# Moving three GpSimd fills ahead of the key and query fills in a hybrid decoder trunk

## The chip, the cores and the metric

The kernel runs on one core of a Trainium2 chip. The metric is the device time of one execution in microseconds, as the median of several runs; the kernel before was run three times. Besides these times there is a trace of one execution, taken by the hardware profiler. In it PE is TensorE's matmuls, PEld its weight loads (they overlap the matmuls), DVE is VectorE, ACT is ScalarE, POOL is GpSimd, and SP is SyncE, whose queue issues nearly all DMAs. "L1217" is line 1217 of the kernel.

## The reference

Two layers of a decoder trunk on 512 tokens plus 16 learned meta tokens (L = 528), with 1024 channels, in float32. Each layer is a mixer and a feed-forward part. The mixer reads one input projection of the normed input and runs three groups beside each other; the change lies in the attention group with its forget gate.

```python
def forgetting_attention(q, k, v, log_f):
    scale = ATTN_HEAD_DIM ** -0.5
    F = jnp.cumsum(log_f, axis=1).transpose(0, 2, 1)

    def attend(start, end):
        qb = q[:, start:end]
        s = jnp.einsum("bqhd,bkhd->bhqk", qb, k[:, :end],
                       preferred_element_type=jnp.float32) * scale
        s = s + F[:, :, start:end, None] - F[:, :, None, :end]
        mask = jnp.arange(start, end)[:, None] >= jnp.arange(end)[None, :]
        s = jnp.where(mask, s, NEG_INF)
        p = jax.nn.softmax(s, axis=-1)
        return jnp.einsum("bhqk,bkhd->bqhd", p.astype(v.dtype), v[:, :end])
    ...

def mixer_sublayer(h, pre_g, post_g, w_in, b_forget, ...):
    u = rms_norm(h, pre_g)
    z = jnp.einsum("bld,de->ble", u, w_in)
    q, k, v, f_logit, a_val, a_gate, sc_b, sc_c, sc_x = jnp.split(z, idx, axis=-1)
    log_f = jax.nn.log_sigmoid((f_logit + b_forget).astype(jnp.float32))
    y_attn = forgetting_attention(q.reshape(hs), k.reshape(hs), v.reshape(hs), log_f)
    a = a_val * jax.nn.sigmoid(a_gate)
    a = causal_depthwise_conv(a, a_dw_w) + a_dw_b
    a = jax.nn.silu(layer_norm(a, a_ln_g, a_ln_b))
    y_conv = jnp.einsum("blc,ce->ble", a, a_pw_w)
    y_sc = sc_b * causal_depthwise_conv(sc_c * sc_x, sc_conv_w)
    y = jnp.concatenate([y_attn, y_conv, y_sc], axis=-1)
    y = jnp.einsum("ble,ed->bld", head_rms_norm(y, head_g), w_out)
    return h + rms_norm(y, post_g)
```

There are 8 heads of 64 channels. The feed-forward part is a gated convolution network with 2816 channels.

## The kernel before

**Tiling.** Channels lie on the 128 partitions, tokens along the free dimension, cut into two halves of 264. Every float32 product is made of three products of rounded parts: a weight is split into a rounded high part (`whi`, a ScalarE cast, L622 in the mixer) and the rest (`wlo`, a VectorE subtraction, L626), the normed input likewise into `uhi` and `ulo`; `mm3` (L650) issues the three matmuls (L656). Weights come through three raw buffers by DMAs on SP's queue (L618).

**Order.** In the mixers the orders of TensorE, ScalarE, VectorE and GpSimd are written out: a planner (`Flow`) holds an estimated duration for each operation, runs threads of TensorE work and queues of work of the other engines against each other in its own time, and issues each instruction when its turn comes. `every` (L1820) names the four engines whose issue order is kept as it is. DMAs on SP's queue pass through the same planner (`flow.op("sp", ...)`), but SP is not in `every`. The setup fills at the head of a mixer are issued directly and have no duration in the planner.

**The mixer around the change** (`mixer`, L944). It opens with the convolution gates and the first products of the short convolution. Then the pool `ap` is opened (L1065) in the memory that the wide weight tiles of the first products used, so that a tile of `ap` waits for the last matmul that reads a weight tile lying there. Its tiles lie in the order of their first mention. In that order of the code GpSimd fills:

- `vals` (L1157 to L1159), the V tiles with their columns of ones;
- `causal` (L1161 to L1164), the mask for the diagonal;
- for each of four head slots, the auxiliary rows of the key tile `kh` (two fills) and of the query tile `qh` (two fills), L1178 to L1184: these rows carry the gate and the maxima through the logits' matmul;
- the first columns of the two `dm` tiles (L1185 to L1189), the diagonal matrices of the maxima;
- `fx` (L1190 and L1191), the forget gate's input, 128 × 5 × 8; `gt` is made there, but not filled;
- the two `p4` tiles (L1195 to L1197), which take the exponentials of the last 16 keys.

Fills through the helper `mset` show as L418.

**Who reads them.** `fill` (L1634) runs the projections in a fixed order: V half 0 with the forget gate's columns (`v_proj`, L1202), then q 0, k 0, a short convolution product, q 1 and so on. `v_proj` makes five tiles of up to 128 tokens (matmuls on L1228), which take turns in three PSUM banks; for each, ScalarE copies V out (L1213) and VectorE adds the bias and writes `fx[:, b, :]` (L1217). A bank is free when both have read it. The thread `forget_gate` (L1244) then follows: ScalarE's Abs, Exp and Ln (L1248 to L1250), VectorE's negative part and sum (L1251, L1253), four additions into `fpre` (L1256), TensorE's prefix sum with two matmuls (L1260 on `fe`, L1261 on `fpre`), VectorE's copy to `gt` (L1262), five transposes (L1270), the split into high and low rows (L1274, L1276), and DMAs of these rows into the key tiles (`gate_rows`, L1287, which show as L533). `maxima` (L1398) reads the key tiles with these rows (L1414).

On VectorE's queue the planner puts the taps of the 31-wide convolution (L972) and of the short one (L1029) between these steps; ScalarE's writes of q and k into their tiles (L1333) and VectorE's of the low parts (L1338) follow the projections.

Of the kernel before, what the change touches and what calls it, by code (L numbers as in the profile page):

```python
# [9 lines left out]
F32 = mybir.dt.float32  # L10
# [5 lines left out]
P = 128  # L16
# [3 lines left out]
N_META = 16  # L20
H = L // 2
DEPTH = 2
HEADS = 8
# [337 lines left out]
def tile_hybrid_trunk(ctx: ExitStack, tc: tile.TileContext, xT, wflat, pv_d, out):  # L361
    nc = tc.nc
# [3 lines left out]
    def T(pool, shape, dt, tag, bufs=None):  # L366
        uid[0] += 1
        kw = {} if bufs is None else {"bufs": bufs}
        return pool.tile(list(shape), dt, tag=tag, name=f"{tag}_{uid[0]}", **kw)
# [47 lines left out]
    def mset(t, val):  # L417
        nc.gpsimd.memset(t.bitcast(F32), val)  # L418
# [525 lines left out]
    def mixer(l, ypool, first, close_first, spans, front=None, rz0=None):  # L944
# [120 lines left out]
        ap = ms.enter_context(tc.tile_pool(name=f"ap{l}", bufs=1, side="right", reuse_waits="tile"))  # L1065
# [91 lines left out]
        vals = T(ap, [P, 5, HEADS, VW], F32, "vals")  # L1157
        mset(vals[:, 4], 0.0)
        mset(vals[:, :, :, DH:], 1.0)  # L1159

        causal = T(ap, [P, 400], BF16, "causal")  # L1161
        nc.gpsimd.memset(causal, 0.0)
# [23 lines left out]
        for j in range(2):  # L1186
            dm = T(ap, [P, L], F32R, f"dm{j}")
            mset(dm[:, :N_META], 0.0)
            dms.append(dm)  # L1189
        fx = T(ap, [P, 5, HEADS], F32, "fx")  # L1190
        nc.gpsimd.memset(fx, 0.0)  # L1191
        gt = T(ap, [P, 5, HEADS], F32, "gt")
        g_hl = [T(mp, [P, L], F32, "sq", 2)[:HEADS].bitcast(F32R) for _ in range(2)]

        p4 = [T(ap, [P, N_META], F32, f"p4{i}") for i in range(2)]  # L1195
        for t in p4:
            mset(t, 0.0)  # L1197


        v_at = {}  # L1200

# [690 lines left out]
    for l in range(DEPTH):  # L1892
# [15 lines left out]
        with ms, tc.manual_schedule(engines=every):  # L1908
            flow.yields = YM
            y, y_at, early = mixer(l, ypool, first, wxs.close, i_spans, front, rz0)  # L1910
# [177 lines left out]
```

## Time and profile before

| | us |
|---|---|
| median of 3 runs | 1301.95 |
| lowest and highest of the 3 | 1300.68 and 1302.20 |
| the profiled execution | 1301.88 |
| its span, first to last instruction | 1300.2 |
| granted TensorE clock, mean of the span | 0.997 of full speed |
| layer 0: from the V products to the gate's rows | about 49.7 to 79 us |
| layer 1: the same | about 696 to 726 us |

A row of a timeline gives the start, the time taken, the engine, the line, the operation with output and inputs, the shape, and in brackets how long the engine had stood idle before and what released it. Rows of one kind that follow each other are merged, with their number behind the x. A row of the waits gives who waited for whom, the total in us, how many times, and the longest. TensorE's matmuls overlap: each is shown with some 0.28 us, while their starts are 0.12 us apart, so lost time is read from the starts.

### The profile page before, as it was taken

To read this page: it belongs to the slowest core of one execution; us is meant where nothing else is said; L and a number is where in the kernel's file an instruction comes from. 1 tells how busy PE (TensorE), PEld (TensorE's weight loads), DVE (VectorE), ACT (ScalarE), POOL (GpSimd) and SP (SyncE) were. 2 spreads that over 40 slices of the span, in tenths; PEclk is the share of its full clock that TensorE was granted. 3 is DMA by queue.
4 is the path that set the end of the run, shared out by engine and by line. 5 is a ranking of instruction groups with operands and counts; after the bars stand their busy time and mean duration, and the time that the engine had idled before them with its cause. 6 is when DMAs were issued, how large, how long until landed. Compare 5 with 4: busy or idle time off the path is not lost. (4 is left out here: it accounts for less than half of the span.)

```text
span 1300.2 us, 23941 instructions
## 1 busy us (share of the span) xinstructions
PE 1278.3 (98%) x9802; PEld 1226.7 (94%) x9802; DVE 852.7 (66%) x1449; ACT 612.2 (47%) x1143; POOL 96.2 (7%) x254
## 2 busy tenths in 40 slices
PE   8999999999999999999989999999999999999997
PEld 8999899999999999999989998899999799989997
DVE  7798765687624663566676877757786256636664
ACT  7254577654423432344662645866543234314443
POOL 1313311000000000000003133100000000000000
PEclk9999999999999999999989999999999999999999
DMA  6136132502232222223340361334032332232321
GB/s 238 34 100 158 50 99 78 201 18 98 82 98 83 96 79 101 95 83 100 105 142 18 108 166 43 97 125 147 18 103 92 97 88 89 72 122 86 92 72 65
DMA packets 46637, 124.75 MB, mean 96 GB/s; under 512 B 5616, under 2 KB 15984, under 8 KB 46528
## 3 DMA queue, kind: packets, MB, share of 16 engines
q1 hardware_dynamic: 46480, 123.10, 30.7%
q8 instruction: 77, 1.26, 0.4%
q14 instruction: 32, 0.26, 0.1%
q0 software_dynamic: 48, 0.13, 0.0%
HBM read 108.04 MB, written 4.33 MB: 86 GB/s over the span
## 5 line engine op out<-in xcount | busy, mean ns | idle before, releaser
L656 PE MATMUL psum<-uhi,whi 128*128 128x264 f32 (+1 forms) x1936 | 454.9, 287 | 2.8 <-ACT uhi L837 1.1
L656 PE MATMUL psum<-ulo,whi 128*128 128x264 f32 (+1 forms) x1936 | 449.2, 285 | 0.8 <-DVE ulo L1869 0.4
L656 PE MATMUL psum<-uhi,wlo 128*128 128x264 f32 (+1 forms) x1936 | 447.3, 284 | 0.0
L656 PEld LDWEIGHTS psum<-uhi,whi 128*128 128x128 f32 x1936 | 324.0, 189 | 8.2 <-issue 1.9
L656 PEld LDWEIGHTS psum<-ulo,whi 128*128 128x128 f32 x1936 | 325.0, 189 | 1.9 <-DVE ulo L1869 0.6
L656 PEld LDWEIGHTS psum<-uhi,wlo 128*128 128x128 f32 x1936 | 324.8, 189 | 0.0
L656 PE MATMUL psum<-yhi,whi 128*128 128x264 f32 (+3 forms) x888 | 247.7, 302 | 1.4 <-ACT yp L2020 1.0
L656 PE MATMUL psum<-yhi,wlo 128*128 128x264 f32 (+3 forms) x888 | 245.4, 299 | 0.7 <-DVE wlo L626 0.7
L656 PE MATMUL psum<-ylo,whi 128*128 128x264 f32 (+3 forms) x888 | 245.0, 298 | 0.0
L508 ACT CAST whi<-raw 128x1024 fp32r<-128x1024 f32 (+1 forms) x110 | 113.3, 1031 | 214.7 <-PE psum L656 200.3
L509 DVE TENSOR_TENSOR wlo<-raw,whi 128x1024 fp32r<-128x1024 f32 (+1 forms) x110 | 132.0, 1200 | 81.7 <-ACT whi L508 79.7
L656 PEld LDWEIGHTS psum<-yhi,whi 128*128 128x128 f32 x888 | 159.0, 188 | 8.7 <-ACT yp L2020 1.4
L656 PEld LDWEIGHTS psum<-yhi,wlo 128*128 128x128 f32 x888 | 159.1, 188 | 6.4 <-DVE wlo L626 1.1
L656 PEld LDWEIGHTS psum<-ylo,whi 128*128 128x128 f32 x888 | 159.3, 188 | 5.4
L1969 DVE SCALAR_TENSOR_TENSOR c<-z,pv,c 128x528 f32<-128x528 f32 (+1 forms) x176 | 131.9, 756 | 2.7
L626 DVE TENSOR_TENSOR wlo<-raw,whi 128x1024 fp32r<-128x1024 f32 (+2 forms) x86 | 102.5, 1204 | 33.6 <-ACT whi L622 30.9
L622 ACT CAST whi<-raw 128x1024 fp32r<-128x1024 f32 (+2 forms) x86 | 87.9, 1030 | 31.1 <-PE psum L656 19.7
L972 DVE SCALAR_TENSOR_TENSOR cacc<-apad,pv,cacc 128x528 f32<-128x528 f32 x120 | 87.6, 771 | 0.2
L1987 ACT CAST yhi<-c 128x528 fp32r<-128x528 f32 (+1 forms) x44 | 27.6, 627 | 108.6 <-DVE c L1983 108.6
L1979 ACT ACTIVATE c<-c 128x528 f32<-128x528 f32 (+1 forms) x44 | 28.1, 639 | 79.3 <-DVE c L1969 79.3
L1967 ACT ACTIVATE c<-z,pv 128x528 f32<-128x528 f32 (+1 forms) x88 | 63.3, 726 | 0.4 <-DVE z L1935 0.4
L1932 DVE TENSOR_TENSOR z<-psum,rz 128x528 f32<-128x528 f32 x40 | 28.3, 708 | 53.7 <-PE psum L656 52.2
(214 smaller groups left out, 1417.2 us busy)
## 6 DMA issues: line engine op xcount, KB each, us to landing
raw<-in_w_dram SPq DMA_DIRECT2D x160, 512.0 KB, 3.6
raw<-in_w_dram SPq DMA_DIRECT2D x32, 448.0 KB, 3.5
h<-in_x_dram SPq DMA_DIRECT2D x16, 264.0 KB
q<-pair_hi SPq DMA_DIRECT2D x24, 132.0 KB, 2.2
k<-pair_hi SPq DMA_DIRECT2D x24, 132.0 KB, 2.4
raw<-in_w_dram SPq DMA_DIRECT2D x4, 528.0 KB, 3.4
h_dram<-h SPq DMA_DIRECT2D x4, 528.0 KB
h<-h_dram SPq DMA_DIRECT2D x8, 264.0 KB, 5.8
```

The source lines that it names most:

```text
L508: nc.scalar.copy(hi[:, :sz], raw[:, :sz])
L509: nc.vector.tensor_sub(lo[:, :sz], raw[:, :sz], hi[:, :sz].bitcast(F32))
L622: nc.scalar.copy(box["hi"][:, :sz], box["raw"][:, :sz])
L626: nc.vector.tensor_sub(lo[:, :sz], box["raw"][:, :sz], box["hi"][:, :sz].bitcast(F32))
L656: nc.tensor.matmul(d, lhsT=w[a][:, k, cols], rhs=rhs(b, k, hf), start=start and i == 0 and p == 0, stop=stop and i == n - 1 and p == 2)
L972: nc.vector.scalar_tensor_tensor(conv[j], in0=src, in1=conv[j], scalar=col("a_dw_w", CK * j + i), op0=ALU.mult, op1=ALU.add)
L1932: nc.vector.tensor_mul(two(t[:, off:]), srcs[0], two(rz))
L1967: nc.scalar.activation(dst, src[:, 2:2 + 2 * fw], AF.Copy, scale=wtap(2, t))
L1969: nc.vector.scalar_tensor_tensor(dst, in0=src[:, i:i + 2 * fw], scalar=wtap(i, t), in1=dst, op0=ALU.mult, op1=ALU.add)
L1979: silu = nc.scalar.activation(cs[0], cs[0], AF.Silu)
L1987: nc.scalar.copy(ghi, cs[0])
```

## The change

The allocation and fill of `fx`, the allocation of `gt`, and the allocation and fills of the two `p4` tiles move from behind the fills of `dm` to a place right behind the fills of `vals`. GpSimd's order becomes vals, fx, p4, causal, keys and queries, dm. The tiles of `ap` between the old and the new place (causal, the key and query tiles, dm) lie 448 bytes further on in every partition. It is done once in each layer's mixer.

```diff
         vals = T(ap, [P, 5, HEADS, VW], F32, "vals")
         mset(vals[:, 4], 0.0)
         mset(vals[:, :, :, DH:], 1.0)
+        fx = T(ap, [P, 5, HEADS], F32, "fx")
+        nc.gpsimd.memset(fx, 0.0)
+        gt = T(ap, [P, 5, HEADS], F32, "gt")
+        p4 = [T(ap, [P, N_META], F32, f"p4{i}") for i in range(2)]
+        for t in p4:
+            mset(t, 0.0)
 
         causal = T(ap, [P, 400], BF16, "causal")
...
             dm = T(ap, [P, L], F32R, f"dm{j}")
             mset(dm[:, :N_META], 0.0)
             dms.append(dm)
-        fx = T(ap, [P, 5, HEADS], F32, "fx")
-        nc.gpsimd.memset(fx, 0.0)
-        gt = T(ap, [P, 5, HEADS], F32, "gt")
         g_hl = [T(mp, [P, L], F32, "sq", 2)[:HEADS].bitcast(F32R) for _ in range(2)]
-
-        p4 = [T(ap, [P, N_META], F32, f"p4{i}") for i in range(2)]
-        for t in p4:
-            mset(t, 0.0)
-
 
         v_at = {}
```

## The prediction

> **What bounds the kernel now.** I read the page's busy shares first, then the waits of the whole trace, then the timelines of GpSimd, VectorE, ScalarE and TensorE around the one wait that touches the moved fills.
>
> ```profile
> span 1300.2 us, 23941 instructions
> PE 1278.3 (98%) x9802; PEld 1226.7 (94%) x9802; DVE 852.7 (66%) x1449; ACT 612.2 (47%) x1143; POOL 96.2 (7%) x254
> ```
>
> TensorE is busy for 98% of the span, so an edit can gain only what TensorE itself stands still for: 1300.2 − 1278.3 = 21.9 us over the whole run, and only the part of it that this edit reaches. The waits show where that part can be. The first row is from the waits of all engines, the others are those of TensorE's weight loads (PEld) and matmuls (PE); the columns are the total in us, the number of times, the longest.
>
> ```profile
> DVE fx L1217 <- POOL p L418: 12.2, 2, 6.3
> PE psum L1261 <- DVE fpre L1256: 1.7, 2, 0.9
> PEld psum L1261 <- DVE fpre L1256: 2.0, 2, 1.0
> PEld psum L1270 <- DVE gt L1262: 0.6, 2, 0.3
> PEld psum L1228 <- DVE fx L1217: 0.3, 2, 0.2
> PEld psum L1414 <- DVE mcol L1421: 1.0, 3, 0.6
> ```
>
> VectorE stands still for 12.2 us, once in each layer's mixer, ahead of the first addition into the forget gate's input tile (fx, L1217), because GpSimd has not filled that tile yet. Three small TensorE waits hang on the same chain: the V products for a bank (L1228), the gate's prefix sum (L1261), the gate's transposes (L1270). GpSimd in layer 0, then VectorE (columns: start, us, engine, line, operation):
>
> ```profile
> 45.65 1.10 POOL L418 MEMSET vals<- 128x528 f32 x2
> ...
> 49.76 1.11 POOL L418 MEMSET q<- 32x528 f32 x2 [1.11 <-PE psum L656]
> ...
> 58.14 0.14 POOL L1191 MEMSET fx<- 128x40 f32 x1
> ```
>
> ```profile
> 46.55 3.52 DVE L972 SCALAR_TENSOR_TENSOR cacc<-apad,pv,cacc 128x528 f32<-128x528 f32 x5
> ...
> 51.60 0.75 DVE L1027 TENSOR_SCALAR sccx<-cxp,pv 128x528 f32<-128x528 f32 x1
> 58.31 0.17 DVE L1217 TENSOR_TENSOR fx<-psum,pv 128x8 f32<-128x8 f32 x1 [5.96 <-POOL p L418]
> ...
> 60.63 2.12 DVE L972 SCALAR_TENSOR_TENSOR cacc<-apad,pv,cacc 128x528 f32<-128x528 f32 x3
> ...
> 68.42 2.34 DVE L626 TENSOR_TENSOR wlo<-raw,whi 128x1024 fp32r<-128x1024 f32 x2
> ...
> 70.90 0.87 DVE L1338 SCALAR_TENSOR_TENSOR q<-psum,q 64x264 fp32r<-64x264 f32 x2
> 71.81 0.77 DVE L1256 TENSOR_TENSOR fpre<-fpre,fe 128x8 f32<-128x8 f32 x4
> ...
> 73.51 1.23 DVE L626 TENSOR_TENSOR wlo<-raw,whi 128x1024 fp32r<-128x1024 f32 x1
> 74.77 0.20 DVE L1262 COPY gt<-psum 128x40 f32<-128x40 f32 x1
> ```
>
> The reader is to see that fx is filled at 58.14, behind all fills of the key and query tiles, and that VectorE's next instruction starts 0.03 us after that fill ends (58.14 + 0.14 = 58.28). ScalarE and TensorE over the same stretch:
>
> ```profile
> 52.78 0.37 ACT L1213 COPY vals<-psum 128x256 f32<-128x256 f32 x1 [2.91 <-PE psum L1228]
> ...
> 64.70 0.36 ACT L1213 COPY vals<-psum 16x256 f32<-16x256 f32 x1 [2.59 <-PE psum L1228]
> 67.14 0.24 ACT L1248 ACTIVATE fe<-fx 128x40 f32<-128x40 f32 x1 [2.07 <-DVE fx L1217]
> 67.28 1.03 ACT L622 CAST whi<-raw 128x1024 fp32r<-128x1024 f32 x1
> ...
> 69.52 0.77 ACT L1333 ACTIVATE q<-psum 64x264 fp32r<-64x264 f32 x2
> 70.50 0.80 ACT L1333 ACTIVATE q<-psum 64x264 fp32r<-64x264 f32 x2 [0.22 <-PE psum L656]
> 71.32 1.05 ACT L622 CAST whi<-raw 128x1024 fp32r<-128x1024 f32 x1
> ```
>
> ```profile
> 58.30 0.28 PE L1228 MATMUL psum<-wlo,uhi 128*128 128x264 f32 x1
> 58.53 0.39 PE L1228 MATMUL psum<-whi,uhi 128*128 128x264 f32 x1
> 58.76 0.28 PE L1228 MATMUL psum<-whi,ulo 128*128 128x264 f32 x1
> 58.88 0.28 PE L1228 MATMUL psum<-wlo,uhi 128*128 128x264 f32 x1
> ...
> 71.39 0.31 PE L1260 MATMUL psum<-fe,tri 128*128 128x40 f32 x2
> 72.63 0.42 PE L1261 MATMUL psum<-fpre,ones_r 128*128 128x40 f32 x2 [0.93 <-DVE fpre L1256]
> ...
> 74.66 0.28 PE L656 MATMUL psum<-uhi,wlo 128*128 128x264 f32 x1
> 75.02 0.71 PE L1270 MATMUL psum<-ident,gt 128*8 128x128 f32 x5
> ```
>
> ScalarE had the last V tile's result at 64.70 but could not start the gate before 67.14, since VectorE, working off what the stop left behind, reached its fifth fx addition only then. Layer 1 repeats it (VectorE's stop is the longest of the two, 6.28):
>
> ```profile
> 705.08 0.17 DVE L1217 TENSOR_TENSOR fx<-psum,pv 128x8 f32<-128x8 f32 x1 [6.28 <-POOL p L418]
> ```
>
> ```profile
> 719.27 0.42 PE L1261 MATMUL psum<-fpre,ones_r 128*128 128x40 f32 x2 [0.80 <-DVE fpre L1256]
> ```
>
> **The change part by part.** No instruction is added or removed; three fills per layer (fx and the two p4 tiles) move ahead of the causal mask and of 16 key and query fills on GpSimd. VectorE's, ScalarE's and TensorE's orders are written out by the planner, whose costs know nothing of these fills, so they stay.
>
> The fx fill itself: it comes behind the two vals fills, which end at 45.65 + 1.10 = 46.75, so it ends near 46.9, 11.3 us earlier than now. VectorE asks for it at 52.35 at the earliest (51.60 + 0.75). Cover 5.4 us; if an added wait used it up, the present state would come back and not a worse one.
>
> What it is moved past: the key, query, mask and dm fills start later by three short fills, of which fx takes 0.14. GpSimd now stands 1.11 us before 49.76 waiting for TensorE, so the delay is taken up there: cost nothing, and it would be about 0.3 us on fills that nobody reads before ScalarE's 69.52 if that wait were gone. No DMA is moved, and none is issued by GpSimd here, so its queue holds nothing else.
>
> Addresses: fx, gt and p4 are 160 + 160 + 2 × 64 = 448 bytes per partition, and the tiles behind them slide by that. Where a key tile then came to lie on other old tiles, a fill could wait as q's first now does, until 49.76; k's first fill is then some 2 us late and GpSimd's row of fills ends near 60.5, still 9 us ahead of 69.52. Between 0 and 2 us on GpSimd, nothing on TensorE; I take 0.
>
> VectorE: the first fx addition moves from 58.31 to about 53.15, behind the V copy on the same bank (52.78 + 0.37). What it has to do until the last V tile is there (64.70) is two L1029 and ten L972 at 0.71 (2.12 / 3) and five fx additions: 12 × 0.71 + 5 × 0.1 = 9.0 us in the 11.5 from 53.15 to 64.7. So VectorE is no longer behind when that tile comes, and the gate's first activation starts at about 65.1 and not at 67.14: the 2.07 of its row go.
>
> TensorE, per layer, three terms:
>
> (a) The bank. The fourth V tile takes the first one's bank, which VectorE frees at 58.4. Starts go 58.30, 58.53, 58.76, 58.88: two steps of 0.23 against 0.12, so 0.22 lost. Both banks' readers would be done by 53.3, five us ahead. 0.22 goes, in either layer: 0.44.
>
> (b) The prefix sum. With the gate 2.0 earlier, the two weight splits (68.42 to 70.7) run from 66.4 to 68.7. The q pair at 70.90 needs ScalarE's pair of 69.52, which needs TensorE's first half of q: 24 products at 0.12 behind the last V tile, about 67.5, and so 68.3. The four fpre additions then run from about 69.8 to 70.6, and now end at 72.58. TensorE reaches L1260 at 71.39 − 0.22 = 71.17 and L1261 some 0.25 later. The wait goes with 0.8 to spare. Its price is 1.7 by the matmuls' row and 2.0 by the weight loads' row for both layers; I take 1.85, the middle.
>
> (c) The transposes. From 74.66 to 75.02 is 0.36 against a step of 0.12, so 0.24 too much. Here the early start no longer helps by itself: ScalarE's second q pair (70.50) waits for TensorE, which is only 0.22 earlier there. So 70.3 to 71.1, VectorE's pair until 72.0, the split until 73.4, the copy of gt until 73.6. TensorE would be there at 74.78 − 0.22 − 1.0 = 73.56. The wait falls from 0.24 to about 0.04; I take 0.2 per layer, 0.4.
>
> Between 73.6 and the next place where VectorE waits for ScalarE and TensorE, everything is earlier by 1.35 to 1.4, so nothing of it is lost there. The sum is 0.44 + 1.85 + 0.4 = 2.7 us. Lower bound 0.44 (only the bank, if ScalarE and not VectorE held the gate), upper bound 5.0 (further VectorE waits, below).
>
> [...] Five to six L972 and L1029 now run while GpSimd fills; while they ran so before (46.55, five in 3.52) one took 0.704, and with GpSimd idle (60.63, three in 2.12) 0.707. [...]
>
> **The rivals.**
>
> *Hidden anyway.* Only the bank's wait goes, and the gate chain is held by something else: the split of weights on ScalarE (67.28) and VectorE, or the q pair. For it: the pair at 70.50 does wait for TensorE. Against it: that pair is needed for (c) only, and L1248 waits 2.07 for fx alone. 1301.88 − 0.44 = 1301.4.
>
> *Given back.* TensorE, 1.4 us ahead, meets a wait that does not move with it, a transfer for instance. For it: TensorE has few free gaps to show that everything behind moves along. Against it: SP's row of gate transfers waits for the gate itself. 1301.9.
>
> *More.* VectorE's later waits shrink too: L1414 for mcol, 1.0 in all, and others of its size. For it: they are VectorE's. Against it: it caught up with TensorE before them. With 1.0 to 2.3 more, 1298.1 to 1296.9.
>
> *The other side: SP's order.* SP is not among the engines whose order is written out (`every` is TensorE, ScalarE, VectorE, GpSimd). Were a weight load, which waits for a split by VectorE, put ahead of the gate's rows, those would be late for the first L1414.
>
> ```profile
> 77.69 0.53 SPq L533 DMA_DIRECT2D k<-sq  x1
> ```
>
> ```profile
> 80.87 0.34 PE L1414 MATMUL psum<-k,q 128*16 128x16 f32 x2
> ```
>
> The row leaves SP at 77.69 and is needed at 80.87: 3.2 us with its landing in it, so between 0 and 2.6 of it is slack. A load held until VectorE's next split, near 82.5, would make it about 5 us late: 2 to 5 us per layer against 1.35 won, so slower from 1.35 us beyond the slack, and 1303 to 1309. Against it: SP's issues have their waits from the same planner, and nothing on SP waits for the moved fills. *That the change doesn't do what it says* (VectorE's wait is laid to the p4 fill behind fx, not to fx) is 1301.9 only if it waited for other fills; p4 moves along.
>
> **How the numbers follow.** The profiled run took 1301.88 (span 1300.2 and 1.7 around it), 0.07 below the median of 1301.95. 1301.88 − 2.7 = 1299.2. Chances: the three waits go, 0.62 (own range 1298.5 to 1299.7); more, 0.13; hidden anyway, 0.12; given back or no effect, 0.07; slower, 0.06. What can be told from no change is 0.2%, 2.6 us, so 1299.35 is the line, and the forecast lies just beyond it: of its 0.62 I count 0.47 below the line. Faster 0.47 + 0.13 = 0.60; within 0.15 + 0.12 + 0.07 = 0.34; slower 0.06. The range takes in most of the further gain and the state in which nothing happens: 1297.2 to 1301.8.
>
> **What would show it.** Right: the row of VectorE waiting 12.2 us for GpSimd gone, fx filled near 46.9, the L1248 wait of 2.07 gone, the PE wait at L1261 gone in both layers, the step before L1270 near 0.16, and a TensorE idle time 2.7 us smaller. (b) is wrong if L1261 still waits for fpre; the order on SP is wrong if the key rows come behind another load and L1414 waits. The prediction as a whole is wrong if these waits go and the first matmuls of the feed-forward part do not start about 1.35 us earlier in layer 0.

## The result and the profile after

The changed kernel takes 1299.58 us (median of 20 runs, 1298.36 to 1300.55) against 1301.87 us of the kernel before on the same chip (20 runs, 1300.68 to 1302.41). The ratio is 0.9982, with a 95% interval of 0.9976 to 0.9989: 2.3 us less, between 1.4 and 3.1. The profiled execution took 1300.55 us, the slowest of its 20, so its own end is a poor guide to a difference of 2 us; the starts of single matmuls are a better one.

Span and busy time of the changed kernel, then its waits (who waited for whom: total us, times, longest):

```profile
span 1298.8 us, 23940 instructions
...
PE 1279.1 (98%) x9802; PEld 1227.8 (95%) x9802; DVE 853.5 (66%) x1449; ACT 612.2 (47%) x1143; POOL 98.5 (8%) x254
```

```profile
DVE fx L1215 <- ACT vals L1211: 7.6, 10, 1.2
...
PEld psum L1268 <- DVE gt L1260: 0.6, 2, 0.3
```

From L1199 on, a line has a number lower by 2 than before. The 12.2 us of VectorE on GpSimd are gone; in their place stand ten short waits on ScalarE's copies of V, 7.6 in all, so VectorE now keeps pace with the V tiles. The prefix sum's wait is gone for matmuls and weight loads. The transposes' wait (L1268) is there as before, 0.6 in all.

The timelines of the changed kernel in layer 0, GpSimd first, then VectorE, ScalarE and TensorE (start, us taken, engine, line, operation, idle before and releaser). The last row shows only the first two of the five transposes, since the stretch shown ends there:

```profile
46.37 0.13 POOL L1161 MEMSET fx<- 128x40 f32 x1
...
49.46 1.10 POOL L418 MEMSET q<- 32x528 f32 x2 [0.44 <-PE psum L656]
...
57.76 0.16 POOL L418 MEMSET dm<- 128x16 f32 x2
```

```profile
52.95 0.17 DVE L1215 TENSOR_TENSOR fx<-psum,pv 128x8 f32<-128x8 f32 x1 [0.91 <-ACT vals L1211]
...
55.88 2.11 DVE L972 SCALAR_TENSOR_TENSOR cacc<-apad,pv,cacc 128x528 f32<-128x528 f32 x3
...
70.81 0.88 DVE L1336 SCALAR_TENSOR_TENSOR q<-psum,q 64x264 fp32r<-64x264 f32 x2 [0.54 <-ACT q L1331]
71.89 1.22 DVE L626 TENSOR_TENSOR wlo<-raw,whi 128x1024 fp32r<-128x1024 f32 x1 [0.20 <-ACT whi L622]
73.14 0.20 DVE L1260 COPY gt<-psum 128x40 f32<-128x40 f32 x1
```

```profile
64.83 0.24 ACT L1246 ACTIVATE fe<-fx 128x40 f32<-128x40 f32 x1 [0.28 <-DVE fx L1215]
...
69.99 0.79 ACT L1331 ACTIVATE q<-psum 64x264 fp32r<-64x264 f32 x2 [2.00 <-PE psum L656]
70.81 1.05 ACT L622 CAST whi<-raw 128x1024 fp32r<-128x1024 f32 x1
```

```profile
57.99 0.28 PE L1226 MATMUL psum<-wlo,uhi 128*128 128x264 f32 x1
58.11 0.29 PE L1226 MATMUL psum<-whi,uhi 128*128 128x264 f32 x1
58.24 0.28 PE L1226 MATMUL psum<-whi,ulo 128*128 128x264 f32 x1
58.36 0.28 PE L1226 MATMUL psum<-wlo,uhi 128*128 128x264 f32 x1
...
70.88 0.31 PE L1258 MATMUL psum<-fe,tri 128*128 128x40 f32 x2
71.02 0.40 PE L1259 MATMUL psum<-fpre,ones_r 128*128 128x40 f32 x2
...
73.01 0.28 PE L656 MATMUL psum<-uhi,wlo 128*128 128x264 f32 x1
73.40 0.38 PE L1268 MATMUL psum<-ident,gt 128*8 128x128 f32 x2
```

Compare these with the same matmuls before. The bank step is gone: 57.99, 58.11, 58.24, 58.36 against 58.30, 58.53, 58.76, 58.88. The lead over before grows there from 0.31 to 0.52 us. (Those first 0.3 us arose at 18 us of the run, ahead of every moved fill, and are no effect of the change.) From L1260, now L1258, to the next matmul it was 72.63 − 71.39 = 1.24 us and is now 71.02 − 70.88 = 0.14: another 1.10, lead 1.61. At the transposes nothing is added: the step was 75.02 − 74.66 = 0.36 and is 73.40 − 73.01 = 0.39.

Layer 1 repeats it, by the row of L1261 before that the prediction shows, which started at 719.27, behind L1260 at 718.16:

```profile
717.67 0.31 PE L1258 MATMUL psum<-fe,tri 128*128 128x40 f32 x2
717.81 0.39 PE L1259 MATMUL psum<-fpre,ones_r 128*128 128x40 f32 x2
```

The step of 1.11 us has become 0.14, a gain of 1.0; the bank step gave 0.2.

### The profile page after: what moved, and what is told of

Read it like the earlier page. It is cut to its first block, busy times and chain, and to the rows that moved or that the text cites. A ratio compares the mean times of both kernels' runs of the same rounds, so it can differ in the third digit from the quotient of the medians.

```text
span 1298.8 us, 23940 instructions
## 1 busy us (share of the span) xinstructions
PE 1279.1 (98%) x9802; PEld 1227.8 (95%) x9802; DVE 853.5 (66%) x1449; ACT 612.2 (47%) x1143; POOL 98.5 (8%) x254
## 5 line engine op out<-in xcount | busy, mean ns | idle before, releaser
L972 DVE SCALAR_TENSOR_TENSOR cacc<-apad,pv,cacc 128x528 f32<-128x528 f32 x120 | 87.6, 770 | 0.2
```

The lines of the kernel that those rows point to most:

```text
L972: nc.vector.scalar_tensor_tensor(conv[j], in0=src, in1=conv[j], scalar=col("a_dw_w", CK * j + i), op0=ALU.mult, op1=ALU.add)
```

## The experiments

All are timed in 5 rounds against the kernel before on the same chip. In the first batch that one took 1302.27 us (33 runs), in the second 1301.55 (18), in the third 1301.76 (21).

**1. Only fx, only p4, only the place in memory, and a less early fill.** The change does three things at once, and the row `POOL p L418` named a p4 fill as VectorE's releaser, not fx. Three kernels take one part each; a fourth fills fx behind the third head's tiles.

e1_fx_only: the kernel before, with the fx and gt lines alone moved.

```diff
         mset(vals[:, :, :, DH:], 1.0)
+        fx = T(ap, [P, 5, HEADS], F32, "fx")
+        nc.gpsimd.memset(fx, 0.0)
+        gt = T(ap, [P, 5, HEADS], F32, "gt")
```

> Only fx (and gt's place) moves ahead of the key and query fills; the p4 tiles stay behind dm. Theory (VectorE's wait is for fx alone): the wait of 12.2 us is gone, L1261 no longer waits for fpre, 1299.4 to 1299.8, as with the whole change. Rival (the p4 fill, which the row of waits names, holds VectorE): 1301.9 and the wait is still there.

e2_p4_only: the p4 lines alone moved.

```diff
         mset(vals[:, :, :, DH:], 1.0)
+        p4 = [T(ap, [P, N_META], F32, f"p4{i}") for i in range(2)]
+        for t in p4:
+            mset(t, 0.0)
```

> Only the two p4 fills move; fx is filled last. Theory: as before, 1301.6 to 1302.1, VectorE's wait at 12 us and now laid to fx itself. Rival (p4 holds VectorE): 1299.6 and no wait.

e3_place_only: all three allocated at the new place, filled at the old one.

```diff
         mset(vals[:, :, :, DH:], 1.0)
+        fx = T(ap, [P, 5, HEADS], F32, "fx")
+        gt = T(ap, [P, 5, HEADS], F32, "gt")
+        p4 = [T(ap, [P, N_META], F32, f"p4{i}") for i in range(2)]
```

> The tiles lie where the changed kernel has them, so causal, the key and query tiles and dm slide by 448 bytes, but the fills stay behind dm as before. Theory (the place in memory does nothing): 1301.6 to 1302.1 with all three TensorE waits of before. Rival (part of the gain is other neighbours in memory): below 1301 with VectorE's wait of 12 us still there.

e4_fx_third: as e3, and fx filled in the loop over the heads.

```diff
             mset(qh[i][0][aux + 32:aux + 64], 0.0)
+            if i == 2:
+                nc.gpsimd.memset(fx, 0.0)
```

> fx is filled behind the third of the four heads' fills, near 55.4 us in layer 0; p4 behind dm. Theory (TensorE loses only what VectorE's 2.7 us of slack between the V tiles, and the 0.8 us between fpre and the prefix sum, do not cover): VectorE still waits some 2.5 to 3 us per layer, yet the bank step and the wait at L1261 are gone and the time is that of the whole change, 1299.4 to 1299.9. Rival (every us of VectorE's wait has its share of the gain): half the gain, 1300.7.

Measured: e1 1299.32 us (11 runs), ratio 0.9976 (0.9967 to 0.9985). e2 1302.10, ratio 0.9998 (0.9989 to 1.0007). e3 1301.97, ratio 0.9994 (0.9985 to 1.0003). e4 1299.54, ratio 0.9980 (0.9971 to 0.9989). The waits of e1, e2, e3 and e4 in this order:

```profile
DVE fx L1217 <- ACT vals L1213: 7.6, 10, 1.2
```

```profile
DVE fx L1216 <- POOL fx L1194: 12.2, 2, 6.3
...
PE psum L1260 <- DVE fpre L1255: 1.7, 2, 0.9
```

```profile
DVE fx L1217 <- POOL p L418: 12.3, 2, 6.3
...
PE psum L1261 <- DVE fpre L1256: 1.7, 2, 0.9
```

```profile
DVE fx L1218 <- POOL fx L1189: 7.5, 2, 3.9
```

The whole gain is the fx fill. With p4 moved away, VectorE waits the same 12.2 us and the row now says fx. Before, p4's fills stood right behind fx's on GpSimd and the row took its name from them, although VectorE did not wait for them: it starts at 58.31, 0.03 us behind the end of the fx fill, and GpSimd's two p4 fills run from 58.21 to 58.37. The slide by 448 bytes does nothing that can be measured. In e4 VectorE still waits up to 3.9 us in a layer, more than the 2.5 to 3 that was expected, and TensorE loses nothing by it. In layer 0 the wait is 3.59:

```profile
55.58 0.17 DVE L1218 TENSOR_TENSOR fx<-psum,pv 128x8 f32<-128x8 f32 x1 [3.59 <-POOL fx L1189]
```

**2. The edge of the cover.** If VectorE's wait is hidden up to some length, then TensorE must pay for each microsecond beyond it. e5 makes the wait longer, e8 and e9 shorten it by little. e5_fx_later: the kernel before, with the four fills of 1.0 in the query tiles made a second time, with the same values, ahead of dm and fx.

```diff
             mset(qh[i][0][aux + 32:aux + 64], 0.0)
+        for i in range(4):
+            aux = rows(i)[1].start
+            mset(qh[i][0][aux:aux + 32], 1.0)
         dms = []
```

> The kernel before, with the first two auxiliary rows' fill of each of the four query tiles made a second time behind the sixteen, ahead of dm and fx: four more fills of 0.55 us, so fx is filled 2.2 us later, near 60.3 us in layer 0. Theory (the three PSUM banks cover about 5.8 us of VectorE's wait, and the kernel before stands just past that edge): every further us is paid in full by TensorE at the fourth V tile, so 2.2 us more per layer, while the wait at L1261 stays near 0.9; 1302.0 + 4.4 = 1306.4. Rival (VectorE's wait is hidden but for the bank step and the prefix sum): 1302 to 1302.6.

e8_fx_one: as e3, and fx filled ahead of the last of the sixteen key and query fills.

```diff
             mset(qh[i][0][aux:aux + 32], 1.0)
+            if i == 3:
+                nc.gpsimd.memset(fx, 0.0)
             mset(qh[i][0][aux + 32:aux + 64], 0.0)
```

> The kernel before with fx filled ahead of the sixteenth fill (and of dm) alone, so some 0.7 us earlier, near 57.45 us in layer 0; p4 behind dm. Theory (the kernel before stands only some 1.3 us beyond the edge of what is covered; up to there each us of VectorE comes off TensorE's waits): the bank step is gone (0.2 per layer), of the 1.1 at L1261 some 0.5 goes and 0.5 to 0.6 stays; 1.4 us in all, 1300.1 to 1300.7 for a kernel before of 1301.9. Rival (the gain needs the fill ahead of all key and query rows): no gain that can be told, 1301.5 to 1302.

e9_fx_two: the same ahead of the last two.

```diff
             mset(kh[i][0][mrow], 1.0)
+            if i == 3:
+                nc.gpsimd.memset(fx, 0.0)
             mset(qh[i][0][aux:aux + 32], 1.0)
```

> The kernel before with fx filled ahead of the last two of the sixteen fills, some 1.25 us earlier, near 56.9 us; p4 behind dm. Theory: nearly the whole gain, 2.3 to 2.5 us, with VectorE still waiting 4.5 to 5 us per layer and at most 0.15 left at L1261; 1299.4 to 1299.7 for a kernel before of 1301.9. Rival as for the run beside it: no more than a tenth of the gain, since 14 of the 16 fills still stand ahead.

Measured: e5 1306.52 us (5 runs), ratio 1.0039 (1.0027 to 1.0052), 5.0 more. e8 1300.35 (11 runs), ratio 0.9990 (0.9981 to 0.9998), 1.4 less. e9 1299.13 (11 runs), ratio 0.9979 (0.9970 to 0.9988), 2.6 less. First the waits of e5, then layer 0 of e5, e8 and e9 (VectorE's first fx addition, and TensorE's two prefix sum matmuls):

```profile
DVE fx L1220 <- POOL p L418: 16.6, 2, 8.5
...
PE psum L1231 <- DVE fx L1220: 4.3, 2, 2.2
...
PE psum L1264 <- DVE fpre L1259: 1.8, 2, 0.9
```

```profile
60.45 0.17 DVE L1220 TENSOR_TENSOR fx<-psum,pv 128x8 f32<-128x8 f32 x1 [8.17 <-POOL p L418]
...
73.55 0.31 PE L1263 MATMUL psum<-fe,tri 128*128 128x40 f32 x2
74.77 0.41 PE L1264 MATMUL psum<-fpre,ones_r 128*128 128x40 f32 x2 [0.91 <-DVE fpre L1259]
```

```profile
57.26 0.17 DVE L1218 TENSOR_TENSOR fx<-psum,pv 128x8 f32<-128x8 f32 x1 [5.20 <-POOL fx L1188]
...
70.90 0.31 PE L1261 MATMUL psum<-fe,tri 128*128 128x40 f32 x2
71.58 0.41 PE L1262 MATMUL psum<-fpre,ones_r 128*128 128x40 f32 x2 [0.37 <-DVE fpre L1257]
```

```profile
56.70 0.17 DVE L1218 TENSOR_TENSOR fx<-psum,pv 128x8 f32<-128x8 f32 x1 [4.74 <-POOL fx L1187]
...
70.80 0.31 PE L1261 MATMUL psum<-fe,tri 128*128 128x40 f32 x2
71.03 0.41 PE L1262 MATMUL psum<-fpre,ones_r 128*128 128x40 f32 x2
```

Put in order of fx, from these rows and those of before, of the changed kernel and of e4 (whose two matmuls start at 70.82 and 70.96). The profiles of before and of e5 are some 0.3 us late from the 18th us of the run on, in both columns alike:

| kernel | VectorE's first fx addition | matmul on fpre | step from the matmul on fe |
|---|---|---|---|
| changed | 52.95 | 71.02 | 0.14 |
| e4 | 55.58 | 70.96 | 0.14 |
| e9 | 56.70 | 71.03 | 0.23 |
| e8 | 57.26 | 71.58 | 0.68 |
| before | 58.31 | 72.63 | 1.24 |
| e5 | 60.45 | 74.77 | 1.22 |

Up to e9 the fx addition may move by 3.75 us and the matmul on fpre stays. From e9 on, the matmul moves with the addition one for one: 0.56 and 0.55, then 1.05 and 1.05, then 2.14 and 2.14. The waits themselves, which know no late start, show where the edge lies. Subtract from VectorE's wait in layer 0 what TensorE pays, the growth of the step at the prefix sum and the loss at the bank: 4.74 − 0.09 in e9, 5.20 − 0.54 in e8, 5.96 − 1.10 − 0.21 before, and 8.17 − 1.08 − 2.42 in e5 (the V products behind the bank fall 2.21 us further back there than the 0.21 of before) all leave 4.65 to 4.67. So 4.65 us of VectorE's wait are covered in layer 0, and TensorE pays for all that goes beyond.

It pays in two places. The banks alone cover more, 5.96 − 0.21 and 8.17 − 2.42, both 5.75 us, near the 5.8 of e5's expectation. Between 4.65 and 5.75 the prefix sum pays, 1.10 us at the most; beyond, the V products wait at the bank (2.2 us in each layer of e5), and the step at the prefix sum grows no further, because everything behind the bank is late by the same amount. The kernel before stands just past both edges.

**3. The transposes.** The term of 0.4 us for L1270 had not come. If the copy of gt is late because it stands behind the weight split on VectorE, ScalarE, which has finished its cast by then, can make it earlier. e6_gt_act: the changed kernel with that one copy on ScalarE. e7_changed_again: the changed kernel once more, to compare with on the same chip.

```diff
-            g = dve(0.25, lambda ps=ps: nc.vector.tensor_copy(gt.rearrange(flat), ps[:, :5 * HEADS]), flow.mm(0.9), prio=0)
+            g = dve(0.25, lambda ps=ps: nc.scalar.copy(gt.rearrange(flat), ps[:, :5 * HEADS]), flow.mm(0.9), prio=0)
```

> The changed kernel, with the copy of the prefix sum into gt made by ScalarE in place of VectorE; all else keeps its order. Theory for the term that did not come (the copy stands behind a weight split on VectorE, which waits for ScalarE's cast and that for the q pair, all of which move with TensorE): ScalarE is free from about 71.9 us, the copy ends near 72.2, and the step before the transposes falls from 0.36 to 0.12 in both layers; 0.5 us less than the changed kernel, 1299.0 to 1299.4. Rival (the transposes wait for the prefix sum's own result): the step stays at 0.36, and the time at that of the changed kernel.

> The changed kernel as it is, beside the two others on the same chip: 1299.3 to 1299.9. If the layer boundary's clock sets part of a run's time, its profile shows TensorE at full speed again at another moment than the first profile's 661.7 us, by up to 1 us, while the steps at L1226 and L1259 are the same to 0.05.

Measured: e6 1298.17 us (8 runs, 1297.15 to 1298.48), ratio 0.9973 (0.9962 to 0.9983). e7 1299.17 (11 runs, 1298.30 to 1299.56), ratio 0.9981 (0.9972 to 0.9990). ScalarE and TensorE in e6:

```profile
70.96 1.05 ACT L622 CAST whi<-raw 128x1024 fp32r<-128x1024 f32 x1
72.03 0.19 ACT L1260 COPY gt<-psum 128x40 f32<-128x40 f32 x1
```

```profile
73.17 0.28 PE L656 MATMUL psum<-uhi,wlo 128*128 128x264 f32 x1
73.29 0.70 PE L1268 MATMUL psum<-ident,gt 128*8 128x128 f32 x5
```

gt is there at 72.03 + 0.19 = 72.22, and the step ahead of the transposes is 0.12 instead of 0.39: 0.27 in layer 0, and 0.29 in layer 1. e6 is the fastest of all kernels here, 1.0 us below e7. The two steps account for 0.56 of it. Its matmuls gain more against the first profile of the changed kernel further on in layer 0, 0.2 us at 90.3 and 0.3 at 139.9, both at matmuls of `maxima` (L1412), whose wait for VectorE's mcol falls from 1.0 to 0.5 us in all; why e6 gains that much there stays open. The intervals of the two ratios overlap, so the 1.0 itself is less sure than the step.

Four medians lie outside what was expected of them, all on the fast side: e1 by 0.1 us, e9 by 0.3, e7 by 0.1 and e6 by 0.8. The steps that were foretold came in all four. In e7 TensorE's full clock behind the layer boundary (last section) came back at 660.06, 1.7 us from the first profile's 661.7 and not within 1.

## Why the prediction was right, and where it was not

The forecast was 1299.2 us, a gain of 2.7; 1299.58 was measured, a gain of 2.3 (1.4 to 3.1), inside the range and inside the likeliest case's own one. Of 2.7, the matmuls' starts show 2.5. That the sum is nearer than its terms is in part luck: (b) was 0.25 too small and (c) 0.4 too large. The time lies 0.2 us above the line of 1299.35 below which the prediction put 0.60 of its chances; that it is a gain is clear of the noise all the same, since the interval of the ratio ends at 0.9989. Of its signs two did not come: the step before the transposes is 0.39 and not near 0.16, and TensorE's idle time fell from 21.9 to 19.7 us, by 2.2 and not 2.7.

*The fx fill and what it is moved past.* fx was expected near 46.9 and the first addition near 53.15; they are at 46.37 + 0.13 = 46.50 and at 52.95, with the run 0.3 us early. The dm fills end at 57.92 instead of 58.22, no later than before but for the 0.3, so the delay was taken up in GpSimd's wait ahead of q, which fell from 1.11 to 0.44, as said. Of these 0.67 only 0.15 are the moved fills; 0.52 are the select of the mask (last section), which the prediction did not foresee and which cost nothing for the same reason. Addresses at nothing: shown by e3.

*VectorE.* It was to be no longer behind when the last V tile comes, with the gate at about 65.1. The gate starts at 64.83 and its wait is 0.28 instead of 2.07. GpSimd's fills beside the taps cost VectorE nothing that shows: three L972 took 2.11 with GpSimd filling throughout (55.88), as they took 2.12 without (60.63 before).

*(a) The bank*, 0.44 forecast: 0.2 per layer, 0.4 in all. Right.

*(b) The prefix sum*, 1.85 forecast: 1.1 and 1.0, so 2.1. The mechanism was right, and e1, e8 and e9 show it at work; the size was low. It was read from the row of the wait, the middle of 1.7 and 2.0. A wait counts from where the engine has finished what it had, and a matmul of 0.31 us that others would have overlapped counts as work: in layer 0 before, 0.31 of matmul and 0.93 of wait make up the step of 1.24. Read from the starts, as (a) and (c) were, it would have been 1.24 − 0.14 = 1.10 in layer 0.

*(c) The transposes*, 0.4 forecast: nothing. This is the step that failed. It said that the copy of gt would come until 73.6, 1.37 earlier than before (74.97), and TensorE at 73.56, 1.22 earlier than its 74.78, so that the wait would nearly close. Measured, the copy ends at 73.34 and TensorE could have started at 73.01 + 0.12 = 73.13: 1.63 and 1.65 earlier, or 1.32 and 1.34 without the 0.31 that the run was early. Both moved alike: the 0.15 between them that the prediction had worked out went to (b), which brought TensorE 0.1 more than was put in, and to small errors in the copy's chain; the 0.2 that it took was finer than its working. It saw that the q pair waits for TensorE, but not that this fixes the wait. In the changed kernel the chain runs from TensorE's q products to ScalarE's second pair (69.99, released by TensorE), the cast (70.81 to 71.86), the split (71.89 to 73.11), the copy (73.14) and the transposes (73.40): 3.41 us, each link within 0.06 us of the one ahead. TensorE itself needs 73.13 − 69.99 = 3.14 from the same release. The difference of 0.27 is a property of the order from there on; an earlier gate cannot touch it. Before, another chain set a wait of nearly the same length: both sides hung on the last fpre addition (71.81 + 0.77 = 72.58), TensorE with the matmul at 72.63, VectorE with its q pair at 72.61, the split at 73.51 and the copy at 74.77. e6 takes the copy out of the chain, and it goes.

*The rivals.* Hidden anyway, 1301.4: refuted, two of three waits went and the gain is beyond 0.44. That the change doesn't do what it says: it does, by e1 and e2. SP's order: it did not come. The gate row to a key tile that left SP at 77.69 now leaves at 76.03, 1.66 earlier, and the matmul that waited for it at 80.87 starts at 79.2: both move along with TensorE. More: the lead over before stays at 1.6 to 1.7 us from the transposes to the end of layer 0, so none of VectorE's later waits gave anything. Given back: in this profile the lead falls from 1.7 to 0.3 us at the layer boundary, 0.7 of it in four matmuls on L793 that ran at half clock (a granted clock of 0.50 from 652.0 on; 2.13 us, before 1.42) and 0.7 because the half clock lasted longer after the restart; TensorE's last transposes (L900) start at 1291.66 instead of 1292.98, only 1.3 earlier, with the 0.3 from the run's start in it. This is the profile and not the change: in e7, the same program, the four matmuls take 1.16 us, the lead falls there from 1.7 to 1.5, and the last transposes start at 1290.44, 2.5 earlier. The medians show 2.3 kept. That a few tenths are given back is not excluded: the interval reaches from 1.4 to 3.1.

## What to carry to other kernels

Order the fills of an engine by when each tile is first needed and not by where the code names it; what a misplaced fill costs is not the wait it causes on an engine with time to spare (12.2 us here) but what of it exceeds the cover (2.5). Price a wait of the bound engine by the starts of its instructions against their usual step, and ask of each remaining wait what releases its chain: if that is the bound engine itself a few microseconds earlier, moving everything forward leaves the wait as it is (the step at the transposes was 0.36 before and 0.39 after). The name in a row of the waits may be that of a neighbour of the one that matters: here it was a fill that had not ended when VectorE started.

## What the runs showed of the hardware

**The clock after the layer boundary.** TensorE waits there for VectorE (2.22 us, ahead of L793) and ScalarE (1.09), and restarts at half clock, a granted 0.50. Windows of the kernel before, of the changed kernel, and of its second run e7 (columns: window, its length, busy time and count of PE, PEld, DVE, ACT, POOL, then granted clock, DMA share, GB/s), each behind the restart's row:

```profile
656.01 0.59 PE L656 MATMUL psum<-uhi,whi 128*128 128x264 f32 x1 [1.09 <-ACT uhi L837]
```

```profile
660.00:661.00 1.00, 1.00 (x6) 1.00 (x6) 1.00 (x2) 0.50 (x1) 0.00 (x0) 0.50 0.00 0
661.00:662.00 1.00, 1.00 (x10) 1.00 (x9) 1.00 (x2) 0.00 (x0) 0.00 (x0) 0.96 0.36 55
```

```profile
655.01 0.59 PE L656 MATMUL psum<-uhi,whi 128*128 128x264 f32 x1 [1.09 <-ACT uhi L837]
```

```profile
661.00:662.00 1.00, 1.00 (x7) 1.00 (x7) 1.00 (x3) 0.00 (x0) 0.00 (x0) 0.64 0.91 338
662.00:663.00 1.00, 1.00 (x10) 1.00 (x9) 1.00 (x2) 0.38 (x1) 0.00 (x0) 1.00 0.92 274
```

```profile
654.02 0.59 PE L656 MATMUL psum<-uhi,whi 128*128 128x264 f32 x1 [1.09 <-ACT uhi L837]
```

```profile
659.00:660.00 1.00, 1.00 (x6) 1.00 (x6) 1.00 (x2) 0.00 (x0) 0.00 (x0) 0.50 0.41 55
660.00:661.00 1.00, 1.00 (x10) 1.00 (x9) 1.00 (x3) 0.00 (x0) 0.00 (x0) 0.97 0.87 334
```

Full clock comes back 5.1 us after the restart in the kernel before (a mean of 0.96 over the microsecond from 661.00 is 0.08 of it at half clock, so at 661.08), 6.7 in the changed kernel and 6.0 in e7, the same program. By the starts of the same matmuls, 0.22 us apart up to there and 0.12 behind it, it took 4.9 us in e6, 6.5 in e9 and 6.6 in e8. So 0.45 of the time at half clock is lost, and by estimate the 1.8 us between e6 and the changed kernel move a run by 0.8 us.

**The mask's select on GpSimd, at 0.29 and at 0.81 us.** The causal mask's select of 128x128 takes 0.29 us in the kernel before and 0.81 in the changed one, where it stands 0.16 us earlier:

```profile
47.18 0.29 POOL L1163 TENSOR_SCALAR_AFFINE_SELECT causal<-causal 128x128 bf16<-128x128 bf16 x1
```

```profile
47.02 0.81 POOL L1169 TENSOR_SCALAR_AFFINE_SELECT causal<-causal 128x128 bf16<-128x128 bf16 x1
```

VectorE ran its convolution taps (L972) in both. What differs is which of the two starts first. In the kernel before, the select starts 0.05 us ahead of a tap (47.18 and 47.23 in layer 0, 693.94 and 693.99 in layer 1) and takes 0.29 in either layer. In the changed kernel a tap has started 0.10 us ahead of it (46.92 and 47.02, 693.72 and 693.82); there it takes 0.81 in either layer and ends 0.15 us behind the end of that tap (47.83 and 47.68, 694.63 and 694.48). VectorE hardly pays: before, the tap that starts behind the select takes 0.81, the next one 0.76; in the changed kernel the tap that starts while the select is still running (47.60) takes 0.79. So the select that comes second takes 0.52 us more, and the tap that comes second 0.05. What holds the select there is not shown.
